# The opening of a hybrid flow-matching step: scratch for squares, loads of the first weights, conditioning rows, and a bound taken in two parts

## The chip, the cores and the metric

The kernel runs on one core of one Trainium2 chip. The metric is the device time of one execution in microseconds, as the median of the runs shown.

## The reference

One layer is computed for two groups of tokens: 2048 sample tokens (conditioning c) and 128 prompt tokens (conditioning c_ctx), D_MODEL 1024.

```python
shift, scale, gate = ada_mod(cvec, w_ada, b_ada)      # silu(cvec) @ w_ada + b_ada, split in three
xn = rmsnorm(h, ln_g) * (1.0 + scale) + shift
proj = jnp.einsum('btd,de->bte', xn, w_in)            # q k v, beta, decay, z_a, u, v, z_b, x_c, z_c, gates
o_a = rmsnorm(o, o_norm_g) * jax.nn.silu(z_a)         # o: bidirectional gated DeltaNet of q, k, v
o_b = chunk_sgu(u_b, v_b, ...) * jax.nn.silu(z_b)
o_c = fourier_mix(x_c, grid) * jax.nn.silu(z_c)
merged = sum over branches of sigmoid(gates) * (o @ w_branch)
h = h + gate * (merged @ w_out);  y = rmsnorm(h, final_g)
```

## The kernel before, in words

All large products run on TensorE in float16 pairs: an operand is held as a high half and a low half (`hi`, `lo`), and a product is three matmuls (hi with hi, hi with lo, lo with hi) that accumulate in PSUM. The scale that brings an operand into float16's range is a power of two from a bound on its size: a sum of squares, summed over the partitions by one small matmul with ones, and then shifted in its bits by VectorE (`scales`, L237 to L247; the copy out of PSUM is L242).

The normed and modulated input is kept in SBUF for the whole kernel as `xh` and `xl`, 128 partitions by 8 tiles of channels (k) by 2176 tokens. It is made in five token blocks (`TBS`): four of 512 and one of 128. The opening has these steps, which the scheduler of the language puts in an order on each engine:

- **Modulation** (`modulate`, L474 to L489). Eleven steps in the order of `ADA_ORDER` read 16 blocks of `w_ada`, half a megabyte each, through the buffers "ab". A block of `ADA_D` is multiplied by VectorE with the conditioning rows `rowc` and summed along the row (L479, one for each group); the others go through TensorE with the conditioning columns `scT` (L220), a copy (L487) and transposes (L489). The rows `rowc` are c and c_ctx, each read to all partitions (half a megabyte each), through a sigmoid (L462) and a product (L463).
- **Block 0** (the sixth step). ScalarE squares the four 128-token pieces of x (`norms`, L453) with the results going to the buffers "xm", which the products L479 use too; VectorE and GpSimd take the reciprocal root (L229, L230); ScalarE scales (L502); TensorE transposes and ScalarE copies eight tiles (L506, L507).
- **The first weights.** `wlist` is the list of weight blocks in the order of use; the first four are those of z_a. `converting` (L265 to L292) is a generator: ScalarE squares into lo (L279), scale, ScalarE makes hi (L291), VectorE lo (L292). Weights are read into two buffers "wst", which are free again when lo is made.
- **The bound** of the modulated input (L530 to L543): `sh` and `ms` from the modulation, ScalarE's squares of both (L537), one scale `sx`.
- **z of block 0** (`silu_za`, L551 to L567): xh by ScalarE (L597), xl by VectorE and GpSimd (L599, L600), z matmuls of weights 1 and 2 in one group, weights 3 and 4 converted by `others` while that group runs, then weights 3 and 4.
- **Blocks 1 to 4** (L580 to L595, L614 to L630): a block's four pieces are read and squared, `row_scale` broadcasts the reciprocal roots by matmuls (L575) and copies them (L577); VectorE multiplies each tile (L586), ScalarE adds the shift (L587, xh), VectorE (L595) or GpSimd (L591, L592) makes xl; then z of the four weights. `row_scale` for the next block is issued behind `made`, the xh instruction of tile 2.

All loads of the opening go through SyncE's queue in the order of the program, one behind the other (`load`, L252 to L261). Behind the opening come the QKV projection, the recurrence of branch A, whose steps are mixed among the matmuls of the other branches (`pace`), and the gated merge.

Of the kernel before, what the change touches and what calls it, by code (L numbers as in the profile page):

```python
# [170 lines left out]
def hybrid_flow_kernel(ctx: ExitStack, tc: tile.TileContext, x_prompt, x_sample, state_delta, c, c_ctx, w_ada,  # L171
# [65 lines left out]
    def scales(ss, pl, tag, sb16=None):  # L237

        ps = bank(ps_x, [P, 1])
        mm(ps, ones16, widened(ss, pl, tag) if sb16 is None else sb16)  # L240
        t = sb(pl, [P, 4], tag)
        V.tensor_copy(t[:, 0:1], ps)  # L242
        h = t[:, 3:4].bitcast(I32)
        V.tensor_scalar(h, t[:, 0:1].bitcast(I32), 24, None, ALU.logical_shift_right)
        V.tensor_scalar(t[:, 1:2].bitcast(I32), h, -8388608.0, 204.0 * 8388608, ALU.mult, ALU.add)
        V.tensor_scalar(t[:, 2:3].bitcast(I32), h, 8388608.0, 50.0 * 8388608, ALU.mult, ALU.add)
        return t[:, 1:2], t[:, 2:3]  # L247
# [20 lines left out]
    def converting(w, st, nkt, cols=P, hi=None, lo=None, tag="w", bufs=5):  # L268

        wpool = bwp[0] if tag == "b" else wp  # L270
        if tag == "z":
            hi, lo = [sb(p0p, [P, nkt, cols], n_, F16, bufs=4) for n_ in ("zhi", "zlo")]
        if tag == "v":
            hi, lo = [t[:, vfilled[0]] for t in v4]
            vfilled[0] += 1
        w.hi = sb(wpool, [P, nkt, cols], tag + "hi", F16, bufs=bufs) if hi is None else hi
        w.lo = sb(wpool, [P, nkt, cols], tag + "lo", F16, bufs=bufs) if lo is None else lo
        ss = sb(wp, [P, 1], "wss", bufs=4)
        A.activation(w.lo, st, AF.Square, accum_out=ss)  # L279
# [11 lines left out]
        w.made = A.activation(w.hi, st, AF.Copy, scale=s)  # L291
        V.scalar_tensor_tensor(w.lo, st, s, w.hi, ALU.mult, ALU.subtract)  # L292

# [142 lines left out]
    isx = None  # L436

    def row_blocks(t0, tn):
        xs = []
        for j in range(tn // P):  # L440
            xs.append(sb(p0p, [P, D], "ab", bufs=9))
            load(xs[-1], xrows(t0 + j * P, P))
        return xs

    def norms(xs, shared=False):
# [11 lines left out]

    rowc = [sb(p0p, [P, D], "ab", bufs=9) for g in range(2)]
# [10 lines left out]
    def ada_load(b):  # L469
        st = sb(p0p, [P, D], "ab", bufs=9)  # L470
        load(st, w_adb[b])
        return st

    def modulate(b):  # L474
        if b in ADA_D:
            st = ada_load(b)
            for g in range(2):
                junk = sb(p0p, [P, D], "xm", F16, bufs=4)
                V.scalar_tensor_tensor(junk, st, 1.0, rowc[g], ALU.mult, ALU.mult, accum_out=ada[:, b, g:g + 1])  # L479
            return  # L480
# [7 lines left out]
        for k in range(2):  # L488
            PE.transpose(pa[:, b + k, :], adr[:, k * P:(k + 1) * P], ident[:2, :2])  # L489

    for i, b in enumerate(ADA_ORDER):
        if i == 3:
            x0 = sb(p0p, [P, 4, D], "xt")
            for j in range(4):
                load(x0[:, j, :], xrows(j * P, P))
        if i > 8:
            read_next()
        modulate(b)
        if i == 5:
            rs0 = norms([x0[:, j, :] for j in range(4)])  # L500
            for j in range(4):
                A.activation(x0[:, j, :], x0[:, j, :], AF.Copy, scale=rs0[:, j:j + 1])  # L502
            for k in range(KT):
                ps = bank(ps_mm, [P, 512])
                for j in range(4):
                    PE.transpose(ps[:, j * P:(j + 1) * P], x0[:, j, k * P:(k + 1) * P], ident)  # L506
                A.copy(raw0[:, k, :], ps)  # L507
# [16 lines left out]
    turn_of[0] = None  # L524
    ms = sb(cp, [P, KT, 2], "ms")
    sh = sb(cp, [P, KT, 2], "sh")
    with tc.high_priority():
        bnd = sb(cp, [P, 2, 2 * KT], "bnd")
        bss = sb(cp, [P, 3], "bss")
        spread = lambda a, n: pc[:, a:a + n].rearrange("p (k o) -> p k o", o=1).to_broadcast([P, n, 2])  # L530
        for i, out in enumerate((sh, ms)):
            n_ = 6 - 2 * i
            V.tensor_tensor(out[:, 0:n_], pa[:, 8 * i:8 * i + n_], spread(49 + 8 * i, n_), ALU.add)
            V.tensor_tensor(out[:, n_:8], ada[:, 8 * i + n_:8 * i + 8], spread(49 + 8 * i + n_, 8 - n_), ALU.add)
            if i:
                V.scalar_tensor_tensor(ms, ms, 1.0, spread(0, 8), ALU.add, ALU.mult)
            A.activation(bnd[:, i, :], flat2(out), AF.Square, scale=math.sqrt(2.0 * D if i else 2.0), accum_out=bss[:, i:i + 1])  # L537
        V.tensor_add(bss[:, 2:3], bss[:, 0:1], bss[:, 1:2])
        sx, isx = scales(bss[:, 2:3], cp, "xsc")
        V.tensor_scalar(ms, ms, sx, None, ALU.mult)  # L540
# [8 lines left out]
    def silu_za(ti, gs, between=None):  # L549
# [4 lines left out]
        for k in range(KT):  # L554
            if k == 5 and between is not None:
                between()
            for g, ps in zip(gs, pss):
# [11 lines left out]
    def row_scale(ti, xs):  # L569

        t0, tn = TBS[ti]
        rs = norms(xs, ti == 1)
        ps = bank(ps_x, [P, len(xs), P])
# [6 lines left out]
    for ti, (t0, tn) in enumerate(TBS):  # L580
        g = 0 if t0 < NS else 1
        for k in range(KT):
            hi, lo = xh[:, k, t0:t0 + tn], xl[:, k, t0:t0 + tn]
            if ti:
                x = xts[ti][:, k, :]
                V.scalar_tensor_tensor(x, x, ms[:, k, g:g + 1], rsb, ALU.mult, ALU.mult)  # L586
# [11 lines left out]
            t = sb(p0p, [P, 512], "xm", bufs=4)  # L598
            of = V.tensor_scalar(t, raw0[:, k, :], ms[:, k, g:g + 1], sh[:, k, g:g + 1], ALU.mult, ALU.add)  # L599
            (V if k % 2 else G).tensor_tensor(lo, t, hi, ALU.subtract)  # L600
        if ti == 0:
            zaw.extend(wdone[:2])
# [7 lines left out]
            with tc.issue_after(zaw[3].made.ins):  # L610
                rsb = row_scale(1, x1)
# [1130 lines left out]
```

## Time and profile before

| | |
|---|---|
| median of 3 runs | 2191.32 us (2187.77 to 2192.63) |
| the profiled execution | 2195.54 us, of which the span of the program's instructions 2193.7 us |
| granted TensorE clock, mean of the span | 0.985 |
| DMA, whole span | 372.96 MB, mean 170 GB/s |
| first z matmul | starts 46.24 us into the span |

The profile's page gives busy times by engine. The waits view says for whom an engine waited: total us, times, longest us. The windows view gives for each stretch the busy us and instruction counts of PE, PEld, DVE, ACT and POOL, then the granted clock, the DMA share and GB/s. A row of the timeline has start, duration, engine, line, operation and tiles, and in brackets the idle time ahead of it and what ended that. A row of the groups view has count, then busy us and mean ns of one, then idle time.

### The profile page before, as it was taken

The numbers are of one execution on the slowest core, as the hardware profiler recorded it, in microseconds if no ns is written. First come the engines' busy times: TensorE is split into PE (matmuls) and PEld (weight loads), VectorE is DVE, ScalarE is ACT, GpSimd is POOL, SyncE is SP. The second block draws the span as 40 slices with busy tenths as digits, with TensorE's granted clock in tenths as the row PEclk, the third lists the DMA queues.
The fourth block names the chain that finished last, engine by engine and source line by source line (L and its number), as shares of the span: only waits on it lengthen the run. The fifth ranks groups of instructions, "written<-read, shape, count | busy, mean of one in ns | idle before, by whom it ended". The sixth has DMA issues, their size and how long they took to land.

```text
span 2193.7 us, 42574 instructions
## 1 busy us (share of the span) xinstructions
PE 2111.5 (96%) x16209; PEld 1204.1 (55%) x16209; DVE 1332.9 (61%) x3150; ACT 1038.5 (47%) x2376; POOL 732.7 (33%) x889
## 2 busy tenths in 40 slices
PE   6799999999999998999899999999999999999998
PEld 2355444455555587778555556555655444444444
DVE  6745955479888697566755556756674544333454
ACT  5634744366555574454544445755553422223332
POOL 1530433133334322443312223355552222122543
PEclk8899999999999999999999999999999999999999
DMA  8524732267777653444655555766764533333543
GB/s 316 230 99 136 292 114 100 75 187 242 243 215 239 200 173 106 117 129 132 211 158 162 155 176 185 241 186 204 223 209 148 172 125 118 129 103 113 178 152 106
DMA packets 228301, 372.96 MB, mean 170 GB/s; under 512 B 38760, under 2 KB 125184, under 8 KB 225664
## 3 DMA queue, kind: packets, MB, share of 16 engines
q1 hardware_dynamic: 175712, 275.24, 39.9%
q0 software_dynamic: 12688, 51.27, 6.4%
q10 hardware_dynamic: 39696, 43.72, 5.9%
q8 instruction: 127, 2.08, 0.4%
q14 instruction: 78, 0.64, 0.1%
HBM read 242.53 MB, written 127.62 MB: 169 GB/s over the span
## 4 chain that ended last, share of the span: by engine, by line
PE 51%; DVE 5%; DMA 4%; ACT 3%; issue 2%; POOL 1%; ACTq 1%; SPq 0%; POOLq 0%; DVEq 0%
PE b L220 50%; DMA wst<-in_w_blk_dram 1%; DMA wst<-in_w_brb_dram 1%; DMA st<-br 1%; ACT nd L902 0%; ACTq L834 0%; DVE big L1520 0%; DMA ei<-XB 0%; DVE wlo L292 0%; DVE XB L949 0%; DVE E L950 0%; PE b L1213 0%; ACTq L839 0%; DMA sk<-kT 0%; DMA ES<-ei 0%
## 5 line engine op out<-in xcount | busy, mean ns | idle before, releaser
L220 PE MATMUL b<-xh,whi 128*128 128x512 f16 (+1 forms) x1920 | 651.7, 348 | 6.1 <-DVE sg L1287 6.0
L220 PE MATMUL b<-xl,whi 128*128 128x512 f16 (+1 forms) x1920 | 652.0, 348 | 0.0
L220 PE MATMUL b<-xh,wlo 128*128 128x512 f16 (+1 forms) x1920 | 651.0, 348 | 0.0
L220 PEld LDWEIGHTS <-whi 128*128 128x128 f16 x3904 | 356.9, 98 | 334.6 <-issue 13.0
L220 PEld LDWEIGHTS <-wlo 128*128 128x128 f16 x1952 | 191.4, 98 | 177.6 <-issue 2.3
L220 PE MATMUL b<-big,bhi 128*128 128x512 f16 (+1 forms) x960 | 251.7, 348 | 4.8 <-ACT big L1519 4.2
L1559 POOL TENSOR_TENSOR mrow<-mrow,sg 128x512 f32<-128x512 f32 (+1 forms) x80 | 94.5, 1182 | 282.9 <-DVE sg L1558 158.9
L220 PE MATMUL b<-big,blo 128*128 128x512 f16 (+1 forms) x480 | 163.5, 348 | 0.0
L1549 ACT ACTIVATE sg<-b,winv 128x512 f32<-128x512 f32 (+1 forms) x120 | 74.2, 619 | 167.5 <-PE b L220 167.1
L220 PEld LDWEIGHTS <-xh 128*128 128x128 f16 x1496 | 118.1, 98 | 35.8 <-issue 5.1
L220 PEld LDWEIGHTS <-bhi 128*128 128x128 f16 x960 | 87.2, 98 | 78.4 <-issue 2.9
L789 POOL TENSOR_TENSOR cy<-cy,raw 128x545 f32<-128x545 f32 (+1 forms) x48 | 67.3, 1429 | 184.2 <-ACT raw L788 184.2
L1558 DVE SCALAR_TENSOR_TENSOR sg<-b,binv,sg 128x512 f32<-128x512 f32 (+1 forms) x80 | 53.5, 668 | 104.6 <-PE b L220 94.8
L234 DVE CAST wscb<-wss 128x1 bf16<-128x1 f32 x93 | 14.2, 153 | 156.0 <-ACT wlo L279 72.6
L220 PE MATMUL b<-whi,xh 128*128 128x128 f16 x544 | 94.3, 221 | 8.1 <-DVE sg L1287 5.0
L220 PE MATMUL b<-wlo,xh 128*128 128x128 f16 x544 | 94.3, 221 | 0.0
L220 PE MATMUL b<-whi,xl 128*128 128x128 f16 x544 | 94.2, 221 | 0.0
L1022 POOL COPY T<-ES 32x256 f16<-32x256 f16 x68 | 29.7, 437 | 192.0 <-DMA ES<-ei 183.6
L220 PE MATMUL b<-wohi,mh 128*128 128x512 f16 (+2 forms) x248 | 91.9, 372 | 0.0
L220 PE MATMUL b<-wolo,mh 128*128 128x512 f16 (+2 forms) x248 | 91.9, 372 | 0.0
L220 PE MATMUL b<-wohi,ml 128*128 128x512 f16 (+2 forms) x248 | 91.7, 372 | 0.0
L292 DVE SCALAR_TENSOR_TENSOR wlo<-wst,wsc,whi 128x1024 f16<-128x1024 f32 x52 | 72.5, 1394 | 25.0 <-ACT whi L291 24.5
(482 smaller groups left out, 4338.8 us busy)
## 6 DMA issues: line engine op xcount, KB each, us to landing
wst<-in_w_blk_dram SPq DMA_DIRECT2D x60, 512.0 KB, 4.1
qkv<-cy POOLq DMA_DIRECT2D x12, 1089.0 KB, 5.2
st<-br SPq DMA_DIRECT2D x48, 256.0 KB, 3.3
mrow<-mrg SPq DMA_DIRECT2D x18, 512.0 KB, 4.4
mrow<-mrg SPq DMA_DIRECT2D x16, 576.0 KB, 3.7
mrg<-mrow POOLq DMA_DIRECT2D x16, 576.0 KB, 3.6
dc<-dec SPq DMA_DIRECT2D x17, 512.0 KB, 5.6
kq<-qkv SPq DMA_DIRECT2D x34, 256.0 KB, 4.8
```

What stands on the lines that cost most here:

```text
L220: PE.matmul(out, l, r, start=start, stop=stop)
L234: V.tensor_copy(sb16, ss)
L292: V.scalar_tensor_tensor(w.lo, st, s, w.hi, ALU.mult, ALU.subtract)
L789: G.tensor_tensor(y[:, c0:c1], y[:, c0:c1], raw[:, 1 + c0:1 + c1], ALU.mult)
L1022: G.tensor_copy(T16[rows(a0, b), :, :, b], ES[0:32, :, 2 * a0 + b, :, wT])
L1549: A.activation(sg, ps, AF.Sigmoid, scale=gw.inv)
L1558: V.scalar_tensor_tensor(sg, ps, binv[:, 1:2], sg, ALU.mult, ALU.mult)
L1559: G.tensor_tensor(mr, mr, sg, ALU.add)
```

## The change

The squares of the first two blocks and the products of the modulation write their unused results to `spare`, two pieces of `xl` that are filled only later, instead of to "xm". The buffers "ab" are seven, not nine. The conditioning rows are made from the columns `scT` by 16 matmuls against the identity and four copies, so c and c_ctx are not read to all partitions, and the sigmoid and product on rows go. Weights 1 and 2 are read ahead of the last two modulation steps, weights 3 and 4 behind the last into "ab" buffers; the order of the last two steps is exchanged. The bound is taken in two parts, `bound(0)` (shift) before the last modulation step, `bound(1)` behind it, and squared by VectorE. The sum of the bound is written in bfloat16 at once, and `scales` shifts straight from PSUM. In block 0 the conversions of weights 3 and 4 begin behind tiles 2 and 4 and go on at fixed places of the first z group. `row_scale` of the next block is issued behind tile 7.

```diff
-ADA_ORDER = (0, 6, 7, 2, 12, 4, 13, 8, 14, 10, 15)
+ADA_ORDER = (0, 6, 7, 2, 12, 4, 13, 8, 14, 15, 10)
...
-        V.tensor_copy(t[:, 0:1], ps)
         h = t[:, 3:4].bitcast(I32)
-        V.tensor_scalar(h, t[:, 0:1].bitcast(I32), 24, None, ALU.logical_shift_right)
+        V.tensor_scalar(h, ps.bitcast(I32), 24, None, ALU.logical_shift_right)
...
-    def read_next():
-        if len(wread) < min(len(wdone) - len(wsteps) + 2, len(wlist)):
+    def read_next(p_=None):
+        if p_ is not None:
+            st = sb(p_, [P, D], "ab", bufs=7).rearrange("p (k c) -> p k c", k=KT)
+            load(st, wlist[len(wread)][0].rearrange("p (k c) -> p k c", k=KT))
+            wread.append(st)
+        elif len(wread) < min(len(wdone) - len(wsteps) + 2, len(wlist)):
...
+    def spare(i):
+        return xl[:, 6 + int(i), 1024:2048]
...
-            jk = sb(p0p, [P, D], "xm", F16, bufs=4)
+            jk = spare(shared and j % 2) if early else sb(p0p, [P, D], "xm", F16, bufs=4)
...
-    for g, src in enumerate((c, c_ctx[None, :])):
-        load(rowc[g], src.to_broadcast([P, D]))
-        sg = sb(p0p, [P, D], "ab", bufs=9)
-        A.activation(sg, rowc[g], AF.Sigmoid)
-        V.tensor_mul(rowc[g], rowc[g], sg)
+    for g in range(2):
+        for half in range(2):
+            ps = bank(ps_mm, [P, 4, P])
+            for k in range(4):
+                mm(ps[:, k, :], scT[:, half * 4 + k, g:g + 1].to_broadcast([P, P]), ident)
+            A.copy(rowc[g][:, half * 512:half * 512 + 512], ps.rearrange("p k c -> p (k c)"))
...
-                junk = sb(p0p, [P, D], "xm", F16, bufs=4)
-                V.scalar_tensor_tensor(junk, st, 1.0, rowc[g], ALU.mult, ALU.mult, accum_out=ada[:, b, g:g + 1])
+                V.scalar_tensor_tensor(spare(1), st, 1.0, rowc[g], ALU.mult, ALU.mult, accum_out=ada[:, b, g:g + 1])
...
+    def bound(i):
+        out, n_ = (ms, 4) if i else (sh, 6)
+        for a, b, src in ((n_, 8, ada[:, 8 * i + n_:8 * i + 8]), (0, n_, pa[:, 8 * i:8 * i + n_])):
...
+        V.scalar_tensor_tensor(bnd[:, i, :], flat2(out), 2.0 * D if i else 2.0, flat2(out), ALU.mult, ALU.mult, accum_out=bss[:, i:i + 1])
...
+        if i == 10:
+            bound(0)
...
-        if i > 8:
+        if i == 9:
+            read_next()
             read_next()
...
+    read_next(p0p)
+    read_next(p0p)
     fetch(2)
     while len(wdone) - len(wsteps) < 2:
         weight_step()
-    read_next()
-    read_next()
...
-                if k == 2:
+                if k == 7:
                     made = act
...
+            if k in (2, 4):
+                fetch(4)
+                begin()
+                with tc.issue_after(made.ins):
+                    next(wsteps[-1])
...
-            def others():
-                with tc.issue_after(made.ins), tc.issue_after(of.ins):
-                    zaw[2:] = getw(4)[2:]
+            def others(k):
+                if k in (4, 5):
+                    for _ in range(2):
+                        next(wsteps[k - 4])
+                if k == 7:
+                    with tc.issue_after(made.ins), tc.issue_after(of.ins):
+                        while wsteps:
+                            next(wsteps.pop(0), 0)
```

Three places show how the scheduler's order moves; line numbers are those of each kernel (L479 of before is L485 now, L292 is L291, L279 is L278, L597 is L610, L577 is L590, L586 is L599, L595 is L608). First VectorE ahead of the first z matmul, before (rows of the scale's bits left out): `wst` and `zlo` are a z weight and its low half, `ab` a modulation block, `adr` the copied result of a modulation step, `bss` and `bs` the bound's sums.

```order
L292 SCALAR_TENSOR_TENSOR zlo_317<-wst_289,wsc_324,zhi_316 128x1024
L479 SCALAR_TENSOR_TENSOR xm_312,ada_120<-ab_310,ab_109 128x1024
L479 SCALAR_TENSOR_TENSOR xm_314,ada_120<-ab_310,ab_110 128x1024
L234 CAST wscb_338<-wss_334 128x1
L487 COPY adr_304<-b_291 2x256
L242 COPY wsc_342<-b_340 128x1
L533 TENSOR_TENSOR sh_366<-b_119,pc_100 128x12
L533 TENSOR_TENSOR ms_365<-b_119,pc_100 128x8
L536 SCALAR_TENSOR_TENSOR ms_365<-ms_365,pc_100 128x16
L292 SCALAR_TENSOR_TENSOR zlo_333<-wst_308,wsc_342,zhi_332 128x1024
L538 TENSOR_TENSOR bss_368<-bss_368 128x1
L234 CAST xscb_378<-bss_368 128x1
```

And now:

```order
L234 CAST wscb_346<-wss_344 128x1
L485 SCALAR_TENSOR_TENSOR xl_94,ada_136<-ab_299,rowc_109 128x1024
L243 TENSOR_SCALAR wsc_350<-b_348 128x1
L291 SCALAR_TENSOR_TENSOR zlo_328<-wst_295,wsc_335,zhi_327 128x1024
L485 SCALAR_TENSOR_TENSOR xl_94,ada_136<-ab_299,rowc_110 128x1024
L244 TENSOR_SCALAR wsc_350<-wsc_350 128x1
L506 TENSOR_TENSOR ms_138<-ada_136,pc_100 128x8
L291 SCALAR_TENSOR_TENSOR zlo_343<-wst_297,wsc_350,zhi_342 128x1024
L493 COPY adr_319<-b_306 2x256
L506 TENSOR_TENSOR ms_138<-b_135,pc_100 128x8
L509 SCALAR_TENSOR_TENSOR bnd_140,bss_141<-ms_138 128x16
L551 TENSOR_TENSOR bs_84_374<-bss_141 128x1
```

Before, the copy of the last modulation result stands ahead of the second weight's zlo; now it stands behind both zlo, with the last two products between the weights' steps.

Second, VectorE between the broadcast of the row scales (`rsb`) of block 2 and the low half of its tiles, before; `xt` is the block's x, transposed.

```order
L577 COPY rsb_722<-b_717 128x512
L586 SCALAR_TENSOR_TENSOR xt_645<-xt_645,ms_365,rsb_722 128x512 x8
L595 SCALAR_TENSOR_TENSOR xl_94<-xt_645,sh_366,xh_93 128x512 x2
L229 TENSOR_SCALAR rs_887<-xss_878 128x4
L595 SCALAR_TENSOR_TENSOR xl_94<-xt_645,sh_366,xh_93 128x512 x2
```

And now, with the silu results `sg` of block 1:

```order
L577 SCALAR_TENSOR_TENSOR sg_684<-b_634,winv_339,sg_684 128x512
L577 SCALAR_TENSOR_TENSOR sg_688<-b_635,winv_354,sg_688 128x512
L590 COPY rsb_709<-b_704 128x512
L599 SCALAR_TENSOR_TENSOR xt_632<-xt_632,ms_138,rsb_709 128x512 x8
L577 SCALAR_TENSOR_TENSOR sg_736<-b_711,winv_461,sg_736 128x512
L608 SCALAR_TENSOR_TENSOR xl_94<-xt_632,sh_139,xh_93 128x512 x4
```

The copy of the row scales now stands behind two silu results of the group of weights 1 and 2, and the low halves behind a third.

Third, ScalarE in block 0, before (`zhi` and `zlo` of a weight, xh the tiles of block 0):

```order
L537 ACTIVATE bnd_367,bss_368<-sh_366 128x16
L291 ACTIVATE zhi_332<-wst_308,wsc_342 128x1024
L537 ACTIVATE bnd_367,bss_368<-ms_365 128x16
L597 ACTIVATE xh_93<-xt_121,sh_366,ms_365 128x512 x8
L279 ACTIVATE zlo_456,wss_457<-wst_336 128x1024
L279 ACTIVATE zlo_473,wss_474<-wst_350 128x1024
L291 ACTIVATE zhi_455<-wst_336,wsc_463 128x1024
L563 ACTIVATE sg_509<-b_423,winv_329 128x512
```

And now:

```order
L610 ACTIVATE xh_93<-xt_137,sh_139,ms_138 128x512 x3
L278 ACTIVATE zlo_400,wss_401<-ab_323 128x1024
L610 ACTIVATE xh_93<-xt_137,sh_139,ms_138 128x512 x2
L278 ACTIVATE zlo_412,wss_413<-ab_325 128x1024
L610 ACTIVATE xh_93<-xt_137,sh_139,ms_138 128x512 x3
L290 ACTIVATE zhi_399<-ab_323,wsc_457 128x1024
L290 ACTIVATE zhi_411<-ab_325,wsc_473 128x1024
```

The squares of weights 3 and 4 stood behind all eight tiles and now stand behind the third and the fifth, and they are read from `ab`.

More of the change, by code (lines that the diff above doesn't have):

```diff
@@ L291, in converting @@
         w.made = A.activation(w.hi, st, AF.Copy, scale=s)
-        V.scalar_tensor_tensor(w.lo, st, s, w.hi, ALU.mult, ALU.subtract)
+        w.low = V.scalar_tensor_tensor(w.lo, st, s, w.hi, ALU.mult, ALU.subtract)
     def convert(st, nkt, *args, **kw):
@@ L456, in norms @@
         return rs
[L458 to L463 removed]
+    rowc = [sb(p0p, [P, D], "rowc") for g in range(2)]
+    for g in range(2):
[4 more added lines that the diff above has]
+            A.copy(rowc[g][:, half * 512:half * 512 + 512], ps.rearrange("p k c -> p (k c)"))
     pa = bank(ps_x, [P, 16, 2])
@@ L489, in modulate @@
             PE.transpose(pa[:, b + k, :], adr[:, k * P:(k + 1) * P], ident[:2, :2])
+    ms = sb(cp, [P, KT, 2], "ms")
+    sh = sb(cp, [P, KT, 2], "sh")
+    bnd = sb(cp, [P, 2, 2 * KT], "bnd")
+    bss = sb(cp, [P, 2], "bss")
+    def bound(i):
+        out, n_ = (ms, 4) if i else (sh, 6)
+        for a, b, src in ((n_, 8, ada[:, 8 * i + n_:8 * i + 8]), (0, n_, pa[:, 8 * i:8 * i + n_])):
+            V.tensor_tensor(out[:, a:b], src, pc[:, 49 + 8 * i + a:49 + 8 * i + b].rearrange("p (k o) -> p k o", o=1).to_broadcast([P, b - a, 2]), ALU.add)
+        if i:
+            V.scalar_tensor_tensor(ms, ms, 1.0, pc[:, 0:8].rearrange("p (k o) -> p k o", o=1).to_broadcast([P, KT, 2]), ALU.add, ALU.mult)
+        V.scalar_tensor_tensor(bnd[:, i, :], flat2(out), 2.0 * D if i else 2.0, flat2(out), ALU.mult, ALU.mult, accum_out=bss[:, i:i + 1])
     for i, b in enumerate(ADA_ORDER):
+        if i == 10:
+            bound(0)
         if i == 3:
@@ L499, in hybrid_flow_kernel @@
         if i == 5:
-            rs0 = norms([x0[:, j, :] for j in range(4)])
+            rs0 = norms([x0[:, j, :] for j in range(4)], early=True)
             for j in range(4):
@@ L524, in hybrid_flow_kernel @@
     turn_of[0] = None
-    ms = sb(cp, [P, KT, 2], "ms")
-    sh = sb(cp, [P, KT, 2], "sh")
     with tc.high_priority():
[L528 to L539, printed above, removed]
+        bound(1)
+        bs16 = sb(cp, [P, 1], "bs16", BF16)
+        V.tensor_add(bs16, bss[:, 0:1], bss[:, 1:2])
+        sx, isx = scales(None, cp, "xsc", bs16)
         V.tensor_scalar(ms, ms, sx, None, ALU.mult)
@@ L554, in silu_za @@
         for k in range(KT):
-            if k == 5 and between is not None:
-                between()
+            if between is not None:
+                between(k)
             for g, ps in zip(gs, pss):
```

21 lines of the change are left out of this document (13 added, 8 removed).

## The prediction

> **What bounds the kernel now.** I read the page first. One execution was profiled, and all sums below stand against it: span 2193.7 us, its own time 2195.54 us, which is 4.2 us above the median of the runs shown (2191.32).
>
> ```profile
> span 2193.7 us, 42574 instructions
> PE 2111.5 (96%) x16209; PEld 1204.1 (55%) x16209; DVE 1332.9 (61%) x3150; ACT 1038.5 (47%) x2376; POOL 732.7 (33%) x889
> ```
>
> TensorE is busy for 96% of the span, so time can only come from where it stands idle or runs at a lower clock. The change lies in the opening, so I read next whom PE waited for in the first 110 us (each row: total, times, longest, us).
>
> ```profile
> PE b L220 <- DMA ab<-in_w_adb_dram: 11.1, 2, 8.8
> PE b L220 <- DVE xl L595: 4.2, 1, 4.2
> PE b L220 <- DVE xscb L234: 3.2, 1, 3.2
> PE b L220 <- DVE zlo L292: 2.9, 1, 2.9
> PE b L220 <- POOL rs L230: 2.5, 1, 2.5
> PE b L220 <- ACT xh L597: 1.9, 1, 1.9
> PE b L220 <- DVE sg L564: 1.5, 1, 1.5
> ```
>
> Then the windows, cut where the granted clock (the figure ahead of the DMA share) changes:
>
> ```profile
> 44.50:51.33 6.83, 5.09 (x13) 1.73 (x13) 6.76 (x15) 5.96 (x9) 3.49 (x3) 0.50 0.96 363
> 51.33:61.57 10.24, 8.22 (x40) 3.57 (x38) 7.01 (x22) 5.48 (x8) 2.85 (x2) 1.00 1.02 419
> 61.57:68.40 6.83, 5.91 (x14) 2.09 (x15) 3.51 (x6) 2.10 (x7) 1.02 (x1) 0.50 1.05 411
> 68.40:82.05 13.65, 9.47 (x49) 4.80 (x48) 9.40 (x16) 7.82 (x14) 3.73 (x2) 1.00 0.82 328
> 82.05:85.46 3.41, 3.41 (x9) 1.18 (x8) 2.78 (x7) 3.41 (x7) 2.30 (x2) 0.50 0.20 77
> 102.53:109.36 6.83, 5.33 (x17) 2.14 (x16) 6.60 (x11) 5.44 (x9) 6.83 (x5) 0.50 0.11 41
> 109.36:180.00 70.64, 70.64 (x643) 38.83 (x642) 29.30 (x71) 25.82 (x46) 19.32 (x25) 1.00 0.24 78
> ```
>
> After each of the idle times of 2.9, 4.2 and 2.5 with 1.5 us the clock is 0.50 for one or two stretches of 3.41 us. A z matmul takes PE 0.21 us at full clock (40 in 8.22 us) and 0.42 at half (14 in 5.91). From 109.36 us on PE is busy without a break. So **the end moves by what changes in three sums**: the start of the first z matmul, the idle times from there to the last token block, and the half-clock stretches behind them.
>
> **The change, part by part.**
>
> *A. Up to the first z matmul.*
>
> ```profile
> 10.00:20.00 10.00, 6.25 (x19) 1.94 (x18) 5.07 (x10) 3.33 (x6) 0.00 (x0) 0.86 1.03 414
> 20.00:30.00 10.00, 10.00 (x39) 3.59 (x38) 6.42 (x12) 2.41 (x4) 3.08 (x1) 0.80 1.02 410
> 8.78 6.07 PE L220 MATMUL b<-ab,scT 128*2 128x256 f32 x16 [8.78 <-DMA ab<-in_w_adb_dram]
> 21.43 1.23 DVE L479 SCALAR_TENSOR_TENSOR xm<-ab,ab 128x1024 f16<-128x1024 f32 x1 [5.09 <-DMA ab<-in_w_adb_dram]
> 22.70 1.06 ACT L453 ACTIVATE xm<-xt 128x1024 f16<-128x1024 f32 x1 [4.53 <-DVE xm L479]
> 25.63 3.08 POOL L230 TENSOR_TENSOR rs<-rs,mhalf 128x4 f32<-128x4 f32 x1 [24.43 <-DVE rs L229]
> 28.74 4.27 ACT L502 ACTIVATE xt<-xt,rs 128x1024 f32<-128x1024 f32 x4 [4.90 <-POOL rs L230]
> 38.83 0.20 ACT L279 ACTIVATION_READ_ACCUMULATOR zlo<-wst 128x1 f32 x1
> 42.54 1.28 DVE L292 SCALAR_TENSOR_TENSOR zlo<-wst,wsc,zhi 128x1024 f16<-128x1024 f32 x1 [1.14 <-ACT zhi L291]
> 43.74 0.15 DVE L538 TENSOR_TENSOR bss<-bss 128x1 f32<-128x1 f32 x1
> 46.24 0.59 PE L220 MATMUL b<-xh,zhi 128*128 128x512 f16 x1 [1.94 <-ACT xh L597]
> ```
>
> The DMA engines are full (1.03, 1.02). The third half-megabyte lands at 8.7 and the thirteenth at 21.4 us: 1.27 us each. Conditioning rows made by matmuls take two of the 24 out of that queue, so everything behind comes 2.5 us earlier: the fourth x block (eighth in the queue) at 15.0, the last modulation block (22nd) at 32.9.
>
> The larger stall is on ScalarE. The fourth square of x waited 4.53 us for a buffer that VectorE's products held; with its scratch in xl it doesn't. In exchange ScalarE makes four copies of 0.59 us of the conditioning rows, and in its new queue the last of them stands behind the first square: first x block 11.2, square 1.1, copy 0.6, so VectorE's second product starts at 13.0. Three products of 1.22 us and a copy later (17.0) the reciprocal root can start; the squares are done by 16.6. With POOL's 3.08 the scaling begins at 20.5 instead of 28.74: **8.2 us earlier**. The 16 small matmuls lie in front of the first modulation block or beside its load; they cost nothing unless PE is late at 20 us, where it is idle.
>
> From there the eight transposed blocks are still copied one by one, with the two squares of z weights now between them (durations in the next rows).
>
> ```profile
> L507 ACT COPY xt<-b 128x512 f32<-128x512 f32 x8 | 4.3, 590 | 1.0 <-PE b L506 1.0
> L279 ACT ACTIVATE zlo<-wst 128x1024 f16<-128x1024 f32 x4 | 4.2, 1049 | 0.0
> L291 ACT ACTIVATE zhi<-wst,wsc 128x1024 f16<-128x1024 f32 x4 | 4.6, 1149 | 4.8 <-DVE wsc L245 4.8
> L479 DVE SCALAR_TENSOR_TENSOR xm<-ab,ab 128x1024 f16<-128x1024 f32 x12 | 14.1, 1220 | 6.8 <-DMA ab<-in_w_adb_dram 6.8
> L292 DVE SCALAR_TENSOR_TENSOR zlo<-wst,wsc,zhi 128x1024 f16<-128x1024 f32 x4 | 5.1, 1282 | 2.6 <-ACT zhi L291 2.6
> ```
>
> Scaling 4.3, copies 8 x 0.59, squares 2 x 1.1, and about 2.1 for PE, which makes each four transposes between modulation matmuls: the second square ends at 33.8 (before: 39.0). What is late next is VectorE's own queue, as the first order fence shows: behind that square stand a product (1.2), zlo of the first weight (1.2), another product (1.2), then the second weight's scale, zhi on ScalarE (1.15) and its zlo (1.2), and only then the copy of the last modulation block, which PE had finished by 35. That is 34.0 + 2 x 1.15 + 1.2 + 0.3 + 1.2 + 1.2 = 40.2. Before, the second zlo ended at 43.8 and the first z matmul followed 2.5 us later; now some nine more small instructions stand between (copy, transposes, sums, the ms half of the bound; 0.15 each by L538's row, 1.3 in all), and a copy and a cast are gone (0.3). First z matmul: 40.2 + 1.3 + 2.2 = 43.7 instead of 46.24. **A = -2.5 us.** Bounds: not earlier than the last modulation block allows (32.9 + 1 of matmuls + 5, so -7), and no gain at all if PE makes the transposes at half clock and each step slips.
>
> The copy that goes in the scale helper is one more such 0.15 us at each use; PE's waits behind 110 us have no row for it, other matmuls cover it, so I take nothing (bounds 0 and -1: a few uses uncovered).
>
> *B. Block 0 and the first half of block 1.* Weights 3 and 4 are now loaded into two of the "ab" buffers, right behind the modulation blocks (landed by 36 us), instead of into buffers that zlo holds, and their two squares lie between the xh tiles (third order fence). For block 0 VectorE has eight scalings, four subtractions and two zlo:
>
> ```profile
> L599 DVE TENSOR_SCALAR xm<-xt,ms,sh 128x512 f32<-128x512 f32 x8 | 4.8, 652 | 0.0
> ```
>
> 5.2 + at most 4 x 1.28 + 2 x 1.28, and two waits for zhi of 1.15: 15.2 us, from a start 0.9 ahead of the first z matmul. PE needs weight 4 after 72 matmuls: 15.1, and 2.6 for the first twelve at half clock. So the wait of 2.9 goes, and with it the half clock at 61.57: 5.91 busy us at half are 2.95 lost. **-5.85.** If VectorE's queue were 3 us longer, the wait would be back.
>
> The wait for xl (4.2) stays. PE needs the lo part of the first tile of block 1 about 9.4 us after the row scales are broadcast:
>
> ```profile
> 72.31 1.05 PE L220 MATMUL b<-cst,rs 128*128 128x128 f32 x8
> 73.40 0.69 DVE L577 COPY rsb<-b 128x512 f32<-128x512 f32 x1 [1.15 <-PE b L220]
> 74.86 5.97 DVE L586 SCALAR_TENSOR_TENSOR xt<-xt,ms,rsb 128x512 f32<-128x512 f32 x7
> 80.87 1.40 DVE L595 SCALAR_TENSOR_TENSOR xl<-xt,sh,xh 128x512 f16<-128x512 f32 x2
> ```
>
> Now 13 matmuls stand behind the broadcast, before 15, and a silu of 0.75 stands ahead on VectorE: the wait grows by 0.9, its half clock by 0.7 (to the 2.4 that the stretches average). **B = -4.25.**
>
> *C. Blocks 2 and 3.* Before, the squares for the next block came after three tiles, and blocks 2 and 3 were prepared early. The waits for rs (2.5) and sg (1.5) and the half clock of 5.33 us behind them go: -6.5 us at most. But now they come after all eight, and the broadcast stands behind the whole double group. The second order fence: after it VectorE has two silus, the copy, eight scalings, one silu, then the lo part. From the end of that group: 0.7 + 0.65 + 0.65 + 0.7 + 6.7 + 0.65 + 0.75 = 10.8 us, while PE has 1.05 + 36 matmuls of 0.21 = 8.6. A wait of 2.2 at block 2; by the same count (0.65 more on VectorE, 0.2 on PE) 2.6 at block 3; each with one half-clock stretch of 3.41, 1.7 lost. +8.2. **C = +1.7.** The eight scalings took 6.7 us beside one POOL instruction in block 1; the same group's mean of 1.0 us is the other end:
>
> ```profile
> L586 DVE SCALAR_TENSOR_TENSOR xt<-xt,ms,rsb 128x512 f32<-128x512 f32 x21 | 19.8, 1003 | 0.0
> ```
>
> At 1.0 each wait is 1.3 longer, so C = +4.3; at the other end the waits don't appear and C = -6.5.
>
> **Sum: -2.5 - 4.25 + 1.7 = -5.05 us**: 2190.5 for a profiled execution like this one, 2186.3 for a median.
>
> The idle times in C are shorter than a stretch of 3.41, and the clock term hangs on that. The 2.9 us wait ahead of 62.5 was followed by 6.83 us at half. By the Trainium skill, TensorE: Matmul & The Clock Gate, section "HAM oscillation — how this bites in real kernels", only idle gaps over about 3.4 us throttle the clock. By that rule C would lose its 3.4 us of clock and the sum be -8.45; the trace disagrees with it at 62.5.
>
> **The rivals.**
>
> 1. *No late waits* (0.13): scalings at 0.66 and matmuls of the neighbouring group that cover the rest; C = -6.5, sum -13.25, 2178.1. Against it: the queue order above.
> 2. *Late waits without half clock* (0.07): a wait of 2 us split over two stretches leaves each busy enough; sum -8.45, 2182.9. Against: 2.5 with 1.5 us were enough at 102.5.
> 3. *Given back* (0.16): transposes at half clock leave A at -1, and C is +4.3 by the group's mean; sum -1 - 4.25 + 4.3 = -0.95, 2190.4.
> 4. *Slower* (0.14): the scheduler has renumbered the whole program; in the recurrence (1447 to 1595 us before) matmuls stand 40 to 130 places from where they stood among the gate matmuls that cover their waits. One uncovered wait has this price:
>
> ```profile
> PE b L220 <- DVE sg L1287: 11.0, 3, 5.0
> 658.90:665.73 6.83, 4.75 (x12) 1.68 (x12) 3.37 (x7) 6.27 (x25) 4.56 (x6) 0.50 0.83 245
> ```
>
> 5.0 us idle and 4.75 busy us at half, 7.4 together. Two of them give 14.8 - 5.05 = +9.75, 2201.1; one gives +2.35, so it is the second that makes it slower. For it: the moves. Against it: PE is busy there without a half-clock stretch, and covering work is left over.
> 5. That scratch or loads don't do what they say needs a hidden wait for xl's low half; the orders show VectorE and ScalarE in different halves, so I give it no chance of its own.
>
> **How the numbers follow.** Forecast 0.50, rivals 0.13, 0.07, 0.16, 0.14. The forecast's own range is 2184 to 2188.5 (1 us on A, 1.3 on C). The range 2178 to 2194 takes in rivals 1 to 3 and one uncovered wait, and leaves out two. A difference of 0.2% (4.4 us) is about what a measurement of this kernel can tell from none: below 2186.9 lie 0.32 of the forecast and rivals 1 and 2, so faster 0.52; same 0.34 (0.18 and rival 3); slower 0.14.
>
> **What would show it.** In the changed profile: scaling of x by ScalarE near 20.5; first z matmul at 43 to 44.5; no PE wait for zlo in block 0; a wait of about 5 for xl at block 1; waits of 2 to 3 at blocks 2 and 3 with half clock behind; unbroken PE from about 104. A first z matmul before 42, no wait at blocks 2 and 3, or a new half-clock stretch after 1400 us would prove a step wrong.

## The result, and the profile after

Over 20 runs each, the kernel before takes 2193.02 us (median) and the changed kernel 2194.82. The ratio is 1.0012, 95% interval 1.0001 to 1.0023: 2.6 us slower, 0.2 to 5.0. The prediction had 2186.3, 5 us under the 2191.32 that three runs of before had given. Below, a difference from before is this ratio, less one, times 2192 us, with the interval. The profiled execution of the changed kernel took 2197.89 us (before: 2195.54).

The head of its page: the span is 2.4 us longer, though the mean granted clock rose from 0.985 to 0.988, and TensorE is busy 1.7 us more.

```profile
span 2196.1 us, 42536 instructions
PE 2113.2 (96%) x16241; PEld 1208.2 (55%) x16241; DVE 1310.1 (60%) x3034; ACT 1039.0 (47%) x2374; POOL 731.5 (33%) x889
```

For whom TensorE waited from 45 to 182 us (total, times, longest):

```profile
PE b L220 <- DVE xl L608: 5.2, 3, 4.2
PE b L220 <- DVE sg L577: 2.4, 2, 1.6
PE b L220 <- ACT xh L610: 1.8, 1, 1.8
PE b L220 <- issue: 1.5, 1, 1.5
```

The waits for zlo (2.9) and rs (2.5) are gone; the waits for xl and sg have become several, and there is one new wait for nothing that the profile shows, at 159 us. The windows where the granted clock (ahead of the DMA share) changes:

```profile
45.42:48.83 3.41, 2.94 (x7) 0.98 (x7) 2.58 (x6) 3.41 (x6) 1.76 (x2) 0.50 0.94 398
48.83:72.72 23.89, 21.21 (x105) 10.15 (x104) 19.82 (x41) 17.21 (x31) 7.48 (x6) 1.00 0.90 341
72.72:79.55 6.83, 5.36 (x13) 1.92 (x13) 6.21 (x9) 5.32 (x10) 6.83 (x5) 0.50 0.34 98
79.55:110.00 30.45, 28.88 (x137) 13.47 (x136) 14.47 (x18) 11.92 (x20) 17.19 (x13) 1.00 0.36 133
161.47:164.88 3.41, 3.41 (x85) 2.54 (x81) 0.90 (x5) 1.22 (x2) 0.00 (x0) 0.50 0.03 7
```

Between 44 and 110 us the clock was at half for 23.9 us before; now it is for 10.2 us. So the opening has become better, much as intended, and yet the whole is slower. The rows of step A:

```profile
18.21 1.02 POOL L230 TENSOR_TENSOR rs<-rs,mhalf 128x4 f32<-128x4 f32 x1 [17.00 <-DVE rs L229]
19.27 4.27 ACT L525 ACTIVATE xt<-xt,rs 128x1024 f32<-128x1024 f32 x4 [1.80 <-POOL rs L230]
26.33 1.56 ACT L530 COPY xt<-b 128x512 f32<-128x512 f32 x3 [2.79 <-PE b L529]
35.95 0.19 ACT L278 ACTIVATION_READ_ACCUMULATOR zlo<-wst 128x1 f32 x1
45.89 0.59 PE L220 MATMUL b<-xh,zhi 128*128 128x512 f16 x1 [1.75 <-ACT xh L610]
```

The scaling starts even earlier than forecast (19.27, not 20.5), but the second square of the z weights ends at 36.1, not 33.8, and the first z matmul starts at 45.89, only 0.35 ahead of before in these two executions.

### The profile page after: what moved, and what is told of

Its sections match the earlier page's. It is cut to its first block, busy times and chain, and to the rows that moved or that the text cites. A ratio compares the mean times of both kernels' runs of the same rounds, so it can differ in the third digit from the quotient of the medians.

```text
span 2196.1 us, 42536 instructions
## 1 busy us (share of the span) xinstructions
PE 2113.2 (96%) x16241; PEld 1208.2 (55%) x16241; DVE 1310.1 (60%) x3034; ACT 1039.0 (47%) x2374; POOL 731.5 (33%) x889
## 5 line engine op out<-in xcount | busy, mean ns | idle before, releaser
L291 DVE SCALAR_TENSOR_TENSOR wlo<-wst,wsc,whi 128x1024 f16<-128x1024 f32 x52 | 70.0, 1347 | 34.4 <-ACT whi L290 34.2
```

The lines of the kernel that those rows point to most:

```text
L291: w.low = V.scalar_tensor_tensor(w.lo, st, s, w.hi, ALU.mult, ALU.subtract)
```

## The experiments

The two traces show a better opening and, from 560 us on, waits that weren't there. One line of the change acts on the whole program: `scales` is used 117 times, and its copy out of PSUM is gone each time. So the first question was whether that line gives the gain back, and then by what: by the shift that reads PSUM, or by the order of instructions, which the scheduler makes anew.

| run | median us | against before, us | interval |
|---|---|---|---|
| changed kernel | 2194.82 | +2.6 | +0.2 to +5.0 |
| e1 copy back | 2182.64 | -10.3 | -12.9 to -7.5 |
| e2 before, no copy | 2204.14 | +10.1 | +7.0 to +12.9 |
| e3 shift first, copy behind | 2183.22 | -8.8 | -11.4 to -5.9 |
| e4 copy unused | 2187.05 | -4.8 | -7.2 to -2.6 |
| e5 copy in the first 24 uses | 2188.01 | -5.0 | -8.8 to -1.3 |
| e6 copy in the first 44 uses | 2185.34 | -8.1 | -11.6 to -4.8 |
| e7 copy in all later uses | 2192.67 | -0.7 | -3.9 to +2.6 |
| e8 copy back, early row scales | 2184.39 | -9.0 | -12.5 to -5.3 |
| e9 ei by SyncE | 2200.6 | +5.9 | +2.8 to +9.0 |
| e10 bdp behind | 2196.86 | +2.6 | -0.4 to +5.7 |
| e11 before, ei by SyncE | 2189.61 | -3.7 | -6.4 to -0.9 |

**e1**, the changed kernel with the line put back:

```diff
+        V.tensor_copy(t[:, 0:1], ps)
-        V.tensor_scalar(h, ps.bitcast(I32), 24, ...)
+        V.tensor_scalar(h, t[:, 0:1].bitcast(I32), 24, ...)
```

> The changed kernel with one line put back: scales copies the sum out of PSUM before it shifts it. The order of instructions behind the opening is then that of before again, almost row for row. Theory ORDER (the opening alone gains about 6 us by the 165th us; the copy's removal moves instructions all over the program, and the waits this makes give about 8 back): 2187, 6 us under before. Theory DIRECT READ (the shift that reads PSUM costs the time, not the order): 2187 too. Theory ABSORBED (whatever the opening gains, later waits on other engines take it back, with either order): 2194 to 2195, like the changed kernel. Theory NO GAIN (the opening gained nothing that lasts, the trace's 6 us is chance of one execution): 2193.

Measured: 10.3 faster than before, 4 more than ORDER had. NO GAIN and ABSORBED are out. In the order of the matmuls in the programs, some 3,700 of 16,161 rows stand more than three places from where they stand in the changed kernel; against before only some 500 do, most of them in the opening and the rest between 814 and 870 us.

**e2**, the opposite edit on the kernel before:

> The kernel before with only the copy in scales removed; the order behind the opening is nearly that of the changed kernel. Theory ORDER and theory DIRECT READ: about 8 us slower than before, 2201. Theory ABSORBED and theory NO GAIN: 2193, like before.

Measured: +10.1. The line costs 10 to 13 us with either opening, and the rest of the change gains about 10; within the intervals the two add up.

**e3**, as many VectorE instructions as before, but the shift reads PSUM:

```diff
-        V.tensor_scalar(h, ps.bitcast(I32), 24, ...)
+        V.tensor_scalar(t[:, 0:1].bitcast(I32), ps.bitcast(I32), 24, ...)
+        V.tensor_copy(h, t[:, 0:1].bitcast(I32))
```

> The changed kernel, where the shift reads PSUM directly and a copy of its result follows, so that there are as many VectorE instructions as in the kernel before and the order is that of e1_copy_back, row for row. Theory ORDER: 2187, like e1. Theory DIRECT READ: 2194 to 2195, like the changed kernel, while e1 stands at 2187. Theory ABSORBED: 2194 to 2195, and e1 too.

Measured: like e1 within the intervals. All 16,161 matmuls stand in e1's order, row for row, and so do the other engines' instructions. DIRECT READ falls: the same read from PSUM, with e1's order, costs nothing that can be told.

**e4**, the copy behind the shift, for nobody:

> The changed kernel with the copy as an unused instruction behind the shift, off the chain: VectorE has the copy's work again, but the order of the other engines is mostly that of the changed kernel. Theory ORDER: 2192 to 2198, like the changed kernel, not like e1. If it were only VectorE's work that counts (a copy more or less), it would be like e1, 2187. Theory DIRECT READ: like the changed kernel, 2195.

Measured: between the two, nearer e1, and better than ORDER had said (2192 to 2198). Its order is a third one, with rows of both, so this fits ORDER only in kind. It speaks against VectorE's extra work as what helps, since e1, e3 and e4 have the same number of copies and differ by 4 to 5 us; the intervals of e3 and e4 overlap.

**e5, e6, e7**, the copy for some of the uses, counted in program order. The order is e1's up to the place and the changed kernel's behind it (e7 the other way round), with one exception: in e5 some 70 matmuls between 814 and 868 us, and the rows of ScalarE and VectorE there, stand as in e1. Nothing else behind 452 us differs from the changed kernel by more than three places.

```diff
+        ncalls.append(0)
+        if len(ncalls) <= 24:              # e5; e6: <= 44; e7: > 44
+            V.tensor_copy(t[:, 0:1], ps)
+            ps = t[:, 0:1]
```

> The changed kernel with the copy in the first 24 uses of scales only (up to about the 450th us): the order on all engines is that of e1_copy_back to about 450 us and that of the changed kernel behind it. e1 took 2182.6 and the changed kernel 2194.8, 12 apart. Theory MIDDLE (from the idle and half-clock times of both traces: 7 of the 12 are lost between 560 and 1060 us, 4 behind that, the rest is chance in the opening): 2193 to 2195. Theory EVEN (each displaced row costs alike, most of them stand at 1360 to 1610 us): 2194. Theory OPENING (the copy counts in the opening and in its first token blocks): 2184.

> The copy in the first 44 uses only: e1's order up to about 1060 us, the changed kernel's behind it. Theory MIDDLE: 2186, 4 over e1. Theory EVEN: 2191, since about two thirds of the displaced matmul rows stand behind 1060 us. Theory OPENING: 2183.

> The complement of e6: no copy in the first 44 uses, the copy in all later ones; the changed kernel's order up to about 1060 us, e1's behind it. Theory MIDDLE: 2190, 7 or 8 over e1. Theory EVEN: 2187. Theory OPENING: 2194. If the two halves add up, e6 and e7 together stand 12 over twice e1.

Measured: 5.3, 2.2 and 9.6 over e1. e6 and e7 together make 11.8, e1's distance to the changed kernel is 12.9, so the halves add up within the intervals. Some 10 us are lost ahead of 1060 us and some 2 behind it. EVEN falls, since most displaced rows stand behind. OPENING is 2 low for e6, 1 high for e7 and 4 low for e5, so the opening isn't all of it; o2 and o3 below give its part as 2.9. MIDDLE was about right for e6 and e7, and wrong for e5, which is 7.6 better than the changed kernel with nearly the same order behind 450 us. The place where the two do differ there says why.

From 700 to 860 us TensorE idles 11.9 us in the changed kernel (160 less 148.06 busy) and has four stretches of 3.41 at half clock; e1 idles 8.3 and has two. First the changed kernel's window, then e1's, then the changed kernel's longest wait there:

```profile
700.00:860.00 160.00, 148.06 (x1541) 108.66 (x1540) 124.86 (x324) 93.17 (x266) 59.58 (x76) 0.96 0.58 177
```

```profile
700.00:860.00 160.00, 151.66 (x1698) 114.22 (x1696) 128.84 (x338) 92.63 (x266) 55.23 (x75) 0.98 0.57 176
```

```profile
PE b L220 <- DVE yT L1500: 4.9, 1, 4.9
```

This wait is at 839 us in the changed kernel; e7 (4.7) and e10 (4.9) have it too, and e4 has one of 4.6 for sg. e5 has none there, and e1 and e6 have 1.4 and 0.9. The kernel before has its own at this place, in a third order of ScalarE:

```profile
PE b L220 <- DVE sg L1287: 5.0, 1, 5.0
```

So e1 gains this wait on both kernels; against before it is no loss. ScalarE's timeline shows its cause. ACTq rows are ScalarE's own issues of writes, with the time that each held its queue. The changed kernel:

```profile
833.44 0.62 ACTq L867 DMA_DIRECT2D ei<-XB  x1
834.10 2.68 ACTq L867 DMA_DIRECT2D ei<-XB  x1
836.82 3.97 ACTq L862 DMA_DIRECT2D n<-n  x1
840.89 0.63 ACT L946 ACTIVATE n<-n 128x512 f16<-128x512 f32 x1 [5.38 <-issue]
840.92 0.90 ACTq L862 DMA_DIRECT2D n<-n  x1
841.86 0.46 ACTq L862 DMA_DIRECT2D qk<-n  x1
842.36 0.37 ACT L1495 COPY us<-b 128x256 f32<-128x256 f32 x1 [0.84 <-DVE n L947]
```

And e1:

```profile
827.93 0.62 ACTq L868 DMA_DIRECT2D ei<-XB  x1
828.04 0.37 ACT L1496 COPY us<-b 128x256 f32<-128x256 f32 x1
828.61 3.05 ACTq L863 DMA_DIRECT2D n<-n  x1
829.81 0.35 ACT L1496 COPY us<-b 128x256 f32<-128x256 f32 x1
831.70 1.18 ACTq L868 DMA_DIRECT2D ei<-XB  x1
833.00 3.25 ACTq L863 DMA_DIRECT2D n<-n  x1
```

In both kernels an issue holds the queue for 3 to 4 us, and ScalarE soon stands idle (the 5.38 that end with "issue"). In e1, and in e5 too, the copies `us` stand ahead of the long issues; in the changed kernel one stands behind five of them, VectorE's yT waits for it, and TensorE for yT.

**e9** takes the two `ei` writes of that place out of ScalarE's queue (**e11** the same in the kernel before):

```diff
-        if g < 4:
+        if g < 3:
             extra.extend(out)
         for o_ in out:
-            if g == 4:
+            if g >= 3:
                 SY.dma_start(*o_)
```

> The changed kernel, where the two half-megabyte writes of the third group's inverse (tile XB to ei, some 835 us into the span) are issued by SyncE and not by ScalarE; rows change between 834 and 900 us only. In the changed kernel ScalarE issues six writes there one behind the other, they take 0.6 to 4.0 us each, the copy us stands behind five of them, and TensorE waits 4.9 us for what VectorE makes of it, with 3.41 us at half clock behind. Theory QUEUE (that wait is ScalarE held up by its own issues): the wait goes, 2188 to 2189, 6 faster than the changed kernel. Theory TRAFFIC (the transfer engines are full there, whoever issues): the wait stays or moves, 2193 to 2196. Either way it is a part of the 12 that the order of e1 spares.

> The kernel before with the edit of e9. Its trace has a wait of 5.2 us at the same place (for the silu result that stands behind four of ScalarE's writes) with 3.41 us at half clock. Theory QUEUE: 5 to 7 faster than before, 2185 to 2187. Theory TRAFFIC: 2190 to 2193.

Measured: e9 is no faster than the changed kernel (3 slower, with intervals that overlap), not 6 faster. The wait at 839 us is gone, which QUEUE had said and TRAFFIC not; but the same edit made another, at 884 us. e9's longest wait from 700 to 1000 us, the half clock there, and what GpSimd did:

```profile
PE b L220 <- POOL X L1484: 8.8, 2, 7.3
```

```profile
887.66:901.32 13.66, 7.36 (x42) 4.26 (x43) 4.54 (x9) 3.16 (x7) 9.67 (x16) 0.50 0.56 169
```

```profile
885.19 0.95 POOL L999 MEMSET R<- 128x1024 f16 x1 [2.84 <-DMA ei<-XB]
887.75 1.81 POOL L999 MEMSET ES<- 128x2048 f16 x1
891.53 0.39 POOL L1484 COPY X<-X 128x252 f16<-128x252 f16 x1
```

GpSimd clears eight tiles once the `ei` writes have landed. In the changed kernel and in before this stands behind the last copies `X`, at 901.15 and 903.80 us; in e9 it stands ahead of some of them, waits 2.84, takes 6.3, and TensorE waits for a copy of 0.39. In e11 the trade is the same in kind: the wait of 5.0 goes and one of 8.2 for that copy comes. Its median still gains 3.7 us, between QUEUE and TRAFFIC, which these two waits don't explain; the profiled execution, 2194.07, was the slowest of its twelve. So the wait at 839 us does hang on those issues, but in e9 moving them doesn't get its price back: the order gives it to another queue.

**e10** moves one row of ScalarE in token block 1:

```diff
-                bdw = convert(bdst, KT, 16, ...)
+                bdw = _W()
+                bdg = converting(bdw, bdst, KT, 16, ...)
+                for _ in range(3):
+                    next(bdg)
...
                 if k == 7:
                     made = act
+                    if ti == 1:
+                        with tc.issue_after(made.ins):
+                            next(bdg, 0)
```

> The changed kernel, where the high half of the small weight bdp is made by ScalarE behind the eight tiles xh of token block 1, not between the first and the second; one row of ScalarE and one of VectorE move, nothing else. Theory ROW (that row is why TensorE's wait for xl in block 1 is 4.5 us with 6.83 us at half clock in the changed kernel, but 3.7 with 3.41 in e1): the wait shrinks by 0.9 and the half clock by one stretch, 2.3 to 2.6 less, 2192.3. Theory OTHER (the wait is set by VectorE's rows, where the order differs too): 2194 to 2195.

Measured: 2196.86, and the wait for xl is unchanged (4.15 in both; the record's 4.5 counts from the start of the matmul ahead, 0.4 more). ROW falls. That e1 and e3 wait less there (3.28) may come from VectorE's rows, which also differ; that wasn't tried.

**e8** takes back the late issue of the row scales alone, and **e12** is the same kernel once more (its label names another edit than it has):

```diff
-                if k == 7:
+                if k == 2:
                     made = act
```

> e1_copy_back with the row scales of the next block issued behind tile 2 again, as before, not behind tile 7; behind the opening the order is that of e1. The prediction's step C priced the late issue at 8.2 (waits of 2.2 and 2.6, each with half clock behind) against 6.5 for the early one: by it 1.7 faster than e1, 2181. By the traces the late waits are there (2.3 and 2.0) but without half clock behind them, and only a wait of 1.7 at 159 us has it: by that the early issue brings back a wait of 4.5 with half clock in 5.3 busy us, and this is 1 to 4 slower than e1, 2184 to 2187.

> e8_copy_back_early_scales once more, one look only: a second profile of the same kernel, to see how far the waits by stage vary from one execution to the next. The idle and half-clock time of each stage (46 to 110, 560 to 700, 700 to 860, 860 to 1000, 1000 to 1115, 1300 to 1460 us) should be within 1.5 us of the first profile's if a stage's waits are set by the order, and differ by 3 us or more if they are chance.

Measured: e8 is 1.3 over e1, too little to tell. e12's single execution took 2183.93, against 2190.29 for e8's profiled one. From 860 to 1000 us, e8 first, then e12:

```profile
860.00:1000.00 140.00, 131.87 (x1791) 107.84 (x1789) 84.76 (x216) 62.27 (x147) 52.00 (x83) 0.96 0.40 117
```

```profile
860.00:1000.00 140.00, 133.32 (x1847) 108.51 (x1845) 88.15 (x224) 63.69 (x151) 53.70 (x88) 0.98 0.42 122
```

Idle and half clock differ by 3.4 us in this stage, 2.4 from 700 to 860, 1.3 or less in the others. One pair of profiles can't place a difference of 3 us; therefore the last four runs time the opening by itself.

**o1 to o4** are cut off behind the QKV projection, all later work left out:

> The kernel before, cut off behind the QKV projection (some 450 us into the span): all later work is left out, and the outputs are filled from the tile xh. The matmuls up to the cut stand in the same order as in the whole kernel. About 470 us; it is the base for o2 to o4.

> The changed kernel, cut off at the same place with the same outputs. Theory SUM (the prediction's three terms): 5.05 under o1. Theory LATE (the whole gain of e1 over before and the whole loss by the copy lie behind the opening): within 1 of o1. From the idle and half-clock time up to 180 us in the traces (before 41.3; after, e4 and e7 30.2 on average, and 5.5 us more of matmul work): 5.6 under o1.

> e1_copy_back, cut off at the same place. Theory SUM (the copy is worth nothing in the opening): like o2. Theory ROWS (the copy's row order counts in the opening too: the traces of e1, e3, e5 and e6 have 26.0 us of idle and half clock up to 180 us, after, e4 and e7 30.2): 4 under o2, 9 to 10 under o1.

> e8_copy_back_early_scales, cut off at the same place: o3 with the row scales issued behind tile 2 again. By the prediction's step C (late issue 8.2 against 6.5): 1.7 under o3. By the traces (27.4 us of idle and half clock up to 180 us in both looks at e8, 26.0 in the kernels with the late issue): 1.4 over o3.

Measured: o1 450.58 (448.04 to 452.88), o2 441.58 (440.90 to 441.78), o3 438.64 (437.49 to 439.22), o4 443.27 (442.36 to 444.68). TensorE's waits from 45 to 130 us, in this order:

```profile
PE b L220 <- DVE xl L595: 4.2, 1, 4.2
PE b L220 <- DVE zlo L292: 2.9, 1, 2.9
PE b L220 <- POOL rs L230: 2.5, 1, 2.5
...
PE b L220 <- DVE sg L564: 1.5, 1, 1.5
```

```profile
PE b L220 <- DVE xl L608: 5.2, 3, 4.2
PE b L220 <- DVE sg L577: 2.4, 2, 1.6
```

```profile
PE b L220 <- DVE xl L609: 4.4, 3, 3.3
PE b L220 <- DVE sg L578: 1.6, 2, 0.9
```

```profile
PE b L220 <- DVE xl L609: 4.1, 1, 4.1
PE b L220 <- POOL rs L230: 3.6, 1, 3.6
PE b L220 <- DVE sg L578: 1.5, 1, 1.5
```

The opening of the changed kernel gains 9.0 us (6 to 12 by the extremes), more than SUM; with the copy back it gains 11.9; and the late issue of the row scales, o3 against o4, gains 4.6, where the record had a loss of 1.7. In the whole kernels it gains only 1.3 (e8 against e1): e1 stands idle for 1.6 at 156 us, with 3.41 at half clock behind, 3.3 together, and e8 and e12 don't. LATE falls. The copy's price of 12.9 is thus 2.9 in the opening (1.7 to 4.3 by the extremes) and about 10 behind it.

## Why the prediction was wrong

**The step that failed** is the one sentence on the copy: "other matmuls cover it, so I take nothing (bounds 0 and -1)". It priced the instruction, and not what its removal does to the order. By e3 neither the read from PSUM nor VectorE's row is what costs; the removal measured +10 to +13 (e2; e1 against the changed kernel). Rival 4 had this mechanism, a new order with uncovered waits, at 0.14, but as an accident of the whole change and with its place in the recurrence at 1447 to 1595 us. The runs place most of it elsewhere, some 10 us ahead of 1060 us. By e5, which differs from the changed kernel in the opening and at 814 to 868 us alone, the 12.9 fall into 2.9 in the opening, some 4.7 at that place (7.6 less 2.9), and 5.3 for the rest of the order (e5 against e1), of which 2.2 stand behind 1060 us; each part is uncertain by 3 to 4 us. What those 5.3 are made of wasn't told apart, and no run has one and the same order with the copy and without.

These places are those of the kernels with the changed opening. In e2, which has the opening of before, the wait at 839 us is 3.1, less than the 5.0 of before, and in its one trace the sum matmul for `qsc`, at the end of the opening, starts at 451.0, against 458.7 in before and 455.8 in e11. So by these traces the loss of 10.1 lies behind 451 us there; which waits make it stays open.

**Step A** (-2.5) was right in kind and somewhat too large. In the cut programs the first z matmul starts at 46.29 (o1) and 44.11 (o2), 2.2 earlier. In all five traces with the changed kernel's opening (the changed kernel, e7, e9, e10, o2) it starts at 43.97 to 45.89, and in the three with that of before (before, e11, o1) at 46.24 to 46.34: 0.4 to 2.4 earlier, so single executions scatter. With the copy back it starts at 42.65 and 42.84 (e1, e3). Two of its numbers were off, in opposite directions, and the second square ended 2.3 later than forecast: POOL's root took 1.02, not 3.08, and ScalarE waited 6.2 us for transposes between its copies (2.79 of it in the row at 26.33), not 2.1, while TensorE had modulation matmuls between the transposes.

**Step B** (-4.25) was right in kind: the wait for zlo went, block 0 runs unbroken to 70.0, and the wait for xl stayed with half clock behind; it is 4.2, as before, where it was to grow to 5.1.

**Step C** (+1.7) had its waits in the right places, at about two thirds of their size, and its clock wrong. At blocks 2 and 3 TensorE stands for 0.8 and 0.8, then 1.6 us, against 2.2 and 2.6 as forecast; and the windows after 98 and 121 us stay at full clock, so the 3.4 us of half clock in the sum didn't come. o2 around 98 and 121 us:

```profile
95.48:98.89 3.41, 1.97 (x9) 0.70 (x8) 3.41 (x5) 3.04 (x6) 3.41 (x4) 1.00 0.12 47
98.89:102.30 3.41, 3.29 (x16) 1.51 (x16) 3.41 (x5) 3.41 (x7) 3.41 (x3) 1.00 0.08 30
119.37:122.78 3.41, 1.60 (x7) 0.56 (x6) 3.41 (x6) 3.04 (x6) 3.41 (x3) 1.00 1.02 405
122.78:126.20 3.42, 3.31 (x16) 1.54 (x16) 3.42 (x7) 1.85 (x3) 3.42 (x3) 1.00 1.03 407
```

And the early issue, had it stayed, would have met the faster opening with a wait of 3.6 for rs instead of 2.5 (o4). So in the cut programs, with the copy back, C is -4.6 where +1.7 was written; this was rival 2's case, at 0.07, whose C of -1.7 was too small as well. A and B, which o4 has without C (and with the copy back), make -7.3 against o1 and were predicted as -2.5 - 4.25 = -6.75.

Two readings in the prediction were slightly off, to no effect: the early issue's waits of 2.5 and 1.5 with half of 5.33 make 6.7, not 6.5; and in rival 4's price the 5.0 is the wait that ends at 846.7 us, while the one ahead of the window at 658.90 took 4.85, so 7.2, not 7.4.

**In sum:** the opening by itself -9.0. In the whole program the changed kernel has, in addition, the 1.5 us of idle time at 159 us and the half-clock stretch behind it (3.41 busy, 1.7 lost), together 3.2, which neither before nor the cut programs have: -5.8. What is left to +2.6 is the new order behind it, about +8.4. The range went up to 2194, about the sum with one uncovered wait of 7.4 on top, and the result lies only 0.8 above it. That it is so near is luck: the opening gained more than the sum had, the order cost more than that one wait, and the base moved up by 1.7, from 2191.32 in three runs to 2193.02 in twenty.

The version that beats both kernels is e1: the change without that line, 2182.64 us, 0.9953 of before (0.9941 to 0.9966).

## What to carry to other kernels

When a scheduler orders the whole program by its own estimate of times, an edit in a helper that is used everywhere isn't priced by its instruction: compare the order far behind the edit, and test the edit alone. An equal number of instructions is no cure by itself: e3 kept the order with it, e4 didn't. Look for engine queues where a cheap copy that TensorE needs can fall behind long DMA issues or a row of memsets; there a place in the order decided over waits of 5 to 8 us. And time a part by a program cut off behind it: here it told 3 us apart in five runs, where one pair of profiles of the whole could not.

## What the runs showed of the hardware

- One issue of a write held ScalarE's queue for 3.97 us, while ScalarE stood idle for 5.38; others of the same size, 4 to 5 us later, took 0.90 and 0.46.
- The half clock does not follow from the length of a wait alone. Waits of 0.8 with 0.8 and of 1.6 us between z matmuls had none behind them in o2, nor had one of 2.3 in e2, while 1.4 with 1.4 had 3.41 us in e2 and 2.9 had 6.83 us in the kernel before. At 155 to 162 us every full-length kernel with the late issue has a stretch of 3.41 at 0.50, all but one behind a wait of 0.9 to 1.7 us in the run of narrow matmuls with `bdp` (16 and 32 columns), and e9 behind no wait at all:

```profile
157.20:160.62 3.42, 3.34 (x134) 3.25 (x131) 0.31 (x1) 1.09 (x4) 0.00 (x0) 1.00 0.13 48
160.62:164.04 3.42, 3.42 (x27) 1.49 (x24) 1.48 (x7) 2.85 (x5) 0.00 (x0) 0.50 0.04 7
```

  By the profile TensorE was busy for 3.34 of the 3.42 us ahead of it, and yet the clock fell. The Trainium skill (TensorE: Matmul & The Clock Gate, section "HAM oscillation — how this bites in real kernels") has gaps of over about 3.4 us as what throttles: the waits of step C agree with it, these rows and the wait of 2.9 don't. What sets the threshold, and what TensorE waited for at 159 us, stays open.
- The 16 conditioning matmuls of 128x128 in f32 are 32 entries in the trace, and take TensorE 6.1 us, most of it ahead of the first modulation block, where it had been idle:

```profile
3.70 4.92 PE L220 MATMUL b<-cst,scT 128*128 128x128 f32 x24 [3.70 <-DVE scT L423]
9.94 1.16 PE L220 MATMUL b<-cst,scT 128*128 128x128 f32 x8
```
